# Sample y with C stationary on column groups, closer norm steps in the last scan unit, and pooling products of half 0 moved into the projection stage

## The chip, the cores and the metric

The kernel runs on one core of one Trainium2 chip. The core has five engines, each with an instruction queue of its own that is worked in order: TensorE (PE; its weight loads are shown as PEld), VectorE (DVE), ScalarE (ACT), GpSimd (POOL) and SyncE (SP), which here issues nearly all DMA transfers. The metric is the device time of one execution in microseconds; less is better. Before the change it is 2911.58 us, the median of 3 runs (2908.11 to 2915.21).

## The reference

One layer of a hybrid decoder trunk is computed in fp32 for 1024 prompt tokens (one sequence) and 64 sample tokens (8 sequences of 8 new tokens, each with a stored state). In short:

```python
x = x + 0.5 * swiglu(rmsnorm(x, norm_ffn1), ffn1_w_in, ffn1_w_out)
proj = rmsnorm(x, norm_mix) @ w_in            # u, z, x/B/C, dt, gate logits
d    = trailing_window_mean(u) - u            # windows 2, 4, 8, 16, one for each group of 256 channels
pool = (einsum('btgc,gcd->btgd', d, w_group) * pool_scale) @ pool_w_out
xs, B, C = silu(causal_conv(x/B/C))
y, state = ssd_scan(xs, dt, A, B, C, h0)      # h_t = exp(dt A) h_{t-1} + dt x_t B_t^T, y_t = h_t C_t
y = (y + d_skip * xs) * silu(z)
y = y * rsqrt(mean of y*y over each of 4 groups + eps) * ssd_norm
x = x + (sigmoid(g0) * pool + sigmoid(g1) * (y @ ssd_w_out)) @ w_o
x = x + 0.5 * swiglu(rmsnorm(x, norm_ffn2), ffn2_w_in, ffn2_w_out)
return rmsnorm(x, norm_final), and the new pool, conv and SSD states
```

The scan has 32 heads of 64 channels in 4 groups of 8 heads; each group has its own B and C of 128 states. For the prompt the state is zero at the start and the scan goes by chunks of 128 tokens. For a sample sequence the state comes in (64 x 128 for each head) and y of its 8 tokens has a part C h0, for each of 8 sequences and 32 heads.

## The kernel before

Activations lie with channels on partitions and tokens along the free dimension. The tokens are in two halves: half 0 is 512 prompt tokens, half 1 is 512 prompt tokens and the 64 sample tokens. A dense product is done in a split form: each fp32 operand is cut into a high and a low part (an ACT copy and a DVE subtraction, `split`), and three products high x high, low x high and high x low are summed in PSUM (`products`, L170 via `mm`). The FFN inputs and most of the projection use a Winograd-like form with seven block products (`wino`, tile pw).

There are four stages, each with its own SBUF and PSUM pools: the first FFN, the projection in its pools, the mix stage (opened by `open_stage("mix", ...)`), and the second FFN. A pool of a stage reuses the space of the one before, so its first tiles wait until the old ones have been read. A shared pool (`act`, 58 buffers of 128 x 576) lives through all of them. PSUM has 8 banks; in the mix stage 4 are for dense products (tag pd) and 4 for all the rest (tag ps).

**Order.** The program is written by a planner. `pe[0]` is its clock: each matmul adds max(columns, 64)/2400 us, four times that in plain fp32, and each transpose adds 0.107. The dense products are written in straight order; beside them run chains (Python generators), which yield a delay: the next piece of a chain is written when the clock has passed its due time (`tick`, `start`). `until(c)` and `finish(c)` write the rest of a chain at once. A list scheduler then fixes each engine's order from that program order and the dependences. Weights that were split and stored earlier (`plan`) are fetched 4 blocks ahead by `load_w` and `part_of`, on SP's queue.

**Mix stage.** The dense line is: pooling's grouped products and its output product for half 0 and half 1 (`mix_pool`, tiles pgm and pbp), the SSD output for half 0 in two parts of 8 rows (`ssd_out(0, 0)`, tile pso, then inside `mix_out(0)` the second part and the product with w_o, tile pwo), the same for half 1, and then the second FFN. Beside it runs the scan as one chain over 8 units (half, group), `scan` and `ssd_group`: for each chunk `ssd_a` (transposes pxT, decays, operand scaling), `ssd_b` (y, tiles pyo and pyd) and the state product pst. In half 1 each unit ends with a fifth chunk for the sample tokens: 8 state blocks (4 head pairs x 2 halves of the batch), each loaded, transposed on PE (ph0T), copied by ACT to h0T, multiplied with C (pyos) and updated with the new tokens' product (pnew).

When a unit ends, `gating` starts as a chain of its own: POOL multiplies with z, ACT squares, DVE adds, PE sums over partitions (pss), DVE takes the inverse root, PE transposes it (prt), it goes to DRAM and comes back on all partitions (rd, r), DVE scales y, and y is stored (yd). The delays between these are GP, G_WAIT and RD_WAIT; `ready[h]` counts stored groups. `y_load(h, q)` waits until the two groups of its part are ready, loads 8 rows of 128 channels and splits them (yh and y); it is started two or four column blocks before the `ssd_out` that uses it.

Before the mix stage, `first_pool` loads the 8 pooled tiles of half 0 (`pool_load`, name dd) and splits them (`pool_cut`, name dh) beside the last gate pair of the projection. In the second FFN, `operands` builds the Winograd operands of each half beside three plain products; T_AT holds the delay of its start, the last two entries for the second FFN.

Of the kernel before, what the change touches and what calls it, by code (L numbers as in the profile page):

```python
# [12 lines left out]
ALU = mybir.AluOpType  # L13
# [40 lines left out]
R_WAIT = 5.0  # L54
F_Y = 0.5
X1_AT = 4.0
T_AT, T_PACE = (2.0, 9.0, 25.0, 2.0), (1.5, 1.5)
DT_AT = 4.0
TURN_WAIT, UST_WAIT = 9.0, 9.0
TURN_AT, CONST_AT = 60.0, 40.0  # L60
HP, HP_ST = 40, 0
N_PRE = 3
Y_PACE = 0.8
G_WAIT = (5.0, 8.0)
H_AT, H_PACE, H_LAND, H_CUT = 1.0, (1.2, 0.9), (7.5, 4.5), 0.9
W_AT, W_NEXT = 108.0, 3.6
AHEAD = 4
# [4 lines left out]
def tile_hybrid_pool_ssd_macaron(  # L72
# [23 lines left out]
    def act(shape=(P, 576), dt=F32, name="a"):  # L96
        return sp.tile(list(shape), dt, tag="act", bufs=N_ACT, name=nm(name))
# [60 lines left out]
    def finish(c):  # L158
        while not c.done:
            c.step()  # L160
# [12 lines left out]
    def tr(out, in_, idn):  # L173
        T.transpose(out, in_, idn)
        pe[0] += 0.107
# [995 lines left out]
    dparts = {}  # L1171

    def pool_load(h, k):
        t = act((P, NTOK[h]), name="dd")
        dma(t, ddd[k][:, slice(*TOK[h])])
        dparts[h, k] = t

    def pool_cut(h, k):
        t = dparts[h, k]
        a = act((P, NTOK[h]), F32R, "dh")  # L1180
        split(t, a, t.bitcast(F32R))
        dparts[h, k] = a, t.bitcast(F32R)

    xn0 = []
    for k in range(KD):
# [45 lines left out]
    c = start(first_pool(), 0.5)  # L1231
    gate_pair(14, (1,))
    finish(c)
    st.close()


# [24 lines left out]
                dma(cdp[hh * HD : (hh + 1) * HD], csrc[hh].partition_broadcast(HD))  # L1261
        return t[:, :n], t[:, 160 : 160 + n], t[:, 320 : 320 + n], cd, (cdp, dtd3)

    def mix_pool(h):

        N, hs = NTOK[h], slice(*TOK[h])
        fh, fl = [None] * KD, [None] * KD

        def group(gi):
            dh, dl = zip(dparts.pop((h, 2 * gi)), dparts.pop((h, 2 * gi + 1)))  # L1270
            for j, pg in enumerate(dense2(wg[gi], 0, 0, [(h, dh, dl)], name="pgm")):
                m = gi * 2 + j
                fh[m], fl[m] = act((P, N), F32R, "fh"), act((P, N), F32R, "fl")
                for pt, (a, b) in zip(pg[0], PIECES[h]):
                    split(pt[:, : b - a], fh[m][:, a:b], fl[m][:, a:b], cols[:, i_ps + m : i_ps + m + 1])

        done = []

        def out(m):
            if done:  # L1280
                later(ACC_AT, lambda d=done.pop(): dma(*d))
            t0 = act((P, N), name="t0")
            dma(t0, gd[m][:, hs])
            pb = dense(wp, 0, KD, m * P, [(h, fh, fl)], name="pbp")[0]
            for pt, (a, b) in zip(pb, PIECES[h]):
                V.scalar_tensor_tensor(t0[:, a:b], t0[:, a:b], 1.0, pt[:, : b - a], op0=ALU.add, op1=ALU.mult)
            done.append((accd[h][m], t0))

        for gi in range(4):
            group(gi)  # L1290
        for m in range(KD):
            if h == 0 and m >= KD - 5:
                for k in range(2 * (m - KD + 5), min(KD, 2 * (m - KD + 5) + 2)):
                    pool_load(1, k)
                if m > KD - 5:
                    for k in range(2 * (m - KD + 4), 2 * (m - KD + 4) + 2):
                        pool_cut(1, k)
            if h == 1 and m == KD - 2:
                loads[0, 0] = start(y_load(0, 0))
            out(m)  # L1300
        dma(*done.pop())
# [40 lines left out]
            out.append((X3, bb))  # L1342
            yield STEP_S

    SAMPLE_UNITS = [(pr, bh) for pr in range(4) for bh in range(2)]

    def state_load(g, i):
        pr, bh = SAMPLE_UNITS[i]
# [67 lines left out]
    def ssd_b(h, g, c, a, hold, Cf, y4, dts, h0s):  # L1416

        dt, acs, dtd, cd, cdp = dts
        ab, xp, xd, ea, btok, L, tok = a[:7]
        smp = c == 4  # L1420
        ysl = y4[:, :, tok]
        first = h == 0 and c == 0
        if smp:
            po = psum("ps", "pyos")
            units, last = SAMPLE_UNITS, []

            def turn(h0, u):
                pt = psum("ps", "ph0T")
                for b in range(4):
                    tr(pt[:, b * P : (b + 1) * P], h0[:, b, :], ident)  # L1430
                hT = act((P, 4, P), name="h0T")
                S.copy(hT.rearrange("p b n -> p (b n)"), pt)
                gp = g * 4 + u[0]
                G.tensor_tensor(h0, h0, cdp[0][:, gp, u[1] * 4 : u[1] * 4 + 4].unsqueeze(2).broadcast_to([P, 4, P]), op=ALU.mult)
                return hT

            hTs = {0: turn(h0s[0], units[0])}
            for i, (pr, bh) in enumerate(units):
                if i + N_H0 < len(units):
                    h0s[i + N_H0] = state_load(g, i + N_H0)  # L1440
                yield STEP_S
                if i + 1 < len(units):
                    hTs[i + 1] = turn(h0s[i + 1], units[i + 1])
                hT, h0 = hTs.pop(i), h0s.pop(i)
                gp = g * 4 + pr
                for b in range(4):
                    bb = bh * 4 + b
                    mm(po[:, pr * L + bb * NT : pr * L + (bb + 1) * NT], hT[:, b, :],
                       Cf[:, 512 + bb * NT : 512 + (bb + 1) * NT])
                pn = psum("ps", "pnew")  # L1450
                mm(pn, xd[bh][0][:, pr * P : (pr + 1) * P], xd[bh][1].rearrange("p b n -> p (b n)"))
                V.tensor_tensor(h0.rearrange("p b n -> p (b n)"), h0.rearrange("p b n -> p (b n)"), pn, op=ALU.add)
                if len(last) > 1:
                    dma(*last.pop(0))
                dst = new_ssm_s[0, bh * 4 : bh * 4 + 4, 2 * gp : 2 * gp + 2].rearrange("b h p n -> (h p) b n")
                last.append((dst, h0))
            yield STEP_S
            for d in last:
                dma(*d)
        elif not first:  # L1460
            po = psum("ps", "pyo")
            for pr in range(4):
                mm(po[:, pr * L : (pr + 1) * L], hold[:, pr * P : (pr + 1) * P], Cf[:, tok])
        py = psum("ps", "pyd")
        for i in range(HPG):
            m_ = ab[:L, i, :]
            mm(py[(i % 2) * HD : (i % 2 + 1) * HD, (i // 2) * L : (i // 2 + 1) * L], xp[:L, i * HD : (i + 1) * HD], m_)
        pyv = py[:, : 4 * L].rearrange("p (q l) -> p q l", l=L)
        if first:
            V.tensor_tensor(ysl, ysl, pyv, op=ALU.add)  # L1470
        else:
            V.tensor_tensor(ea, po[:, : 4 * L].rearrange("p (q l) -> p q l", l=L), ea, op=ALU.mult)
            V.tensor_tensor(ea, ea, pyv, op=ALU.add)
            G.tensor_tensor(ysl, ysl, ea, op=ALU.add)

# [52 lines left out]
    def gating(h, g, y4, z4):  # L1528

        N = NTOK[h]  # L1530
        for j in range(4):
            G.tensor_tensor(y4[:, j, :N], z4[j], y4[:, j, :N], op=ALU.mult)
        yield GP[0]
        sq = [act((P, N), name="sq") for _ in range(4)]
        for j in range(4):
            S.activation(sq[j], y4[:, j, :N], AF.Square)
        yield GP[2]
        for j in range(1, 4):
            V.tensor_tensor(sq[0], sq[0], sq[j], op=ALU.add)
        sums = sq[:1]  # L1540
        rr = []
        yield from rstd(None, h, 512, rr, 1.0, sums, G_WAIT, RD_WAIT)
        for j in range(4):
            k = g * 4 + j
            y = y4[:, j, :N]
# [14 lines left out]

    def y_load(h, q):

        while ready[h] < 2 * q + 2:
            yield 1.0
        N = NTOK[h]
        parts = [], []
        for k in range(8 * q, 8 * q + 8):
            t, a = act((P, N), name="y"), act((P, N), F32R, "yh")
            dma(t, yd[h][k])
            parts[0].append(a)  # L1570
            parts[1].append(t)
            yield Y_LOAD
        yield 3.0
        for i in range(9):
            if i < 8:
                S.activation(parts[0][i], parts[1][i], AF.Copy)
            if i:
                a, t = parts[0][i - 1], parts[1][i - 1]
                V.tensor_tensor(t.bitcast(F32R), t, a.bitcast(F32), op=ALU.subtract)
            yield Y_PACE  # L1580
        return h, parts[0], [t.bitcast(F32R) for t in parts[1]]

    def scan():
# [97 lines left out]
        prep2.append((start(norm_parts(reload(0), 0, i_g2, o, PACE)), o))  # L1681
        return prep2[0][0]

    for h in HALVES:
        plan += [(w, 0, 2, 0, 2 * P) for w in wg]
        plan += [(wp, kb, 4, m * P, P) for m in range(KD) for kb in (0, 4)]
    for h in HALVES:
        plan += [(ws, q + kb, 4, m * P, P) for q in (0, 8) for m in range(KD) for kb in (0, 4)]
        plan += [(wz, kb, 4, m * P, P) for m in range(KD) for kb in (0, 4)]
    for h in HALVES:  # L1690
        plan += [(wi2, kb, 4, c0 + ff * P, P) for ff in range(N_PLAIN) for kb in (0, 4) for c0 in (0, FF)]
    start(scan())
    mix_pool(0)
    mix_pool(1)
    ssd_out(0, 0, (0, 1))
    mix_out(0, lambda: None, None)
    ssd_out(1, 0, (1, 1))
# [125 lines left out]
```

## Time and profile before

| | |
|---|---|
| median of 3 runs | 2911.58 us (2908.11 to 2915.21) |
| profiled execution, its own time | 2908.95 us |
| its span, first to last instruction | 2907.0 us |
| mean granted TensorE clock | 0.990 |
| PE busy | 2836.2 us, 98% of the span |
| DVE, ACT, POOL busy | 1635.7, 1316.6, 853.9 us |
| mix stage, from the last gate pair to the second FFN | about 1480 to 2150 us |

In the page and the views behind it, a row such as `PE MATMUL pyos<-Cf,h0T x256` names the engine, the operation, the tile written and the tiles read; buffer numbers are left out. An fp32 product shows as two records (two passes). Waits name what released an engine. In the view of busy time by stretch the column PEclk is the share of TensorE's full clock that was granted. In the chain of waits each line is a start, a length and what ran or was waited for.

### The profile page before, as it was taken

To read this page: it belongs to the slowest core of one execution; us is meant where nothing else is said; L and a number is where in the kernel's file an instruction comes from. 1 tells how busy PE (TensorE), PEld (TensorE's weight loads), DVE (VectorE), ACT (ScalarE), POOL (GpSimd) and SP (SyncE) were. 2 spreads that over 40 slices of the span, in tenths; PEclk is the share of its full clock that TensorE was granted. 3 is DMA by queue.
4 is the path that set the end of the run, shared out by engine and by line. 5 is a ranking of instruction groups with operands and counts; after the bars stand their busy time and mean duration, and the time that the engine had idled before them with its cause. 6 is when DMAs were issued, how large, how long until landed. Compare 5 with 4: busy or idle time off the path is not lost.

```text
span 2907.0 us, 54116 instructions
## 1 busy us (share of the span) xinstructions
PE 2836.2 (98%) x20338; PEld 2684.4 (92%) x20338; DVE 1635.7 (56%) x2839; ACT 1316.6 (45%) x2756; POOL 853.9 (29%) x913
## 2 busy tenths in 40 slices
PE   7999999999999999999999999999999999999998
PEld 6999999889999999999987887779999999998898
DVE  6556666544366877676458756762365433345532
ACT  5445545433244465555567745551223333344422
POOL 5333334110053333344214333431124333340100
PEclk9999999999999999999999999999999999999999
DMA  4489987755453333323378887886774222235542
GB/s 141 144 285 310 301 281 250 247 170 156 147 157 112 103 108 99 121 90 104 118 239 297 300 298 246 297 307 215 266 237 138 75 79 75 82 103 198 185 126 73
DMA packets 530520, 528.93 MB, mean 182 GB/s; under 512 B 43386, under 2 KB 372208, under 8 KB 530250
## 3 DMA queue, kind: packets, MB, share of 16 engines
q1 hardware_dynamic: 521846, 498.56, 53.0%
q0 software_dynamic: 7040, 24.52, 2.4%
q8 instruction: 160, 2.62, 0.4%
q10 hardware_dynamic: 1372, 2.40, 0.2%
q14 instruction: 102, 0.84, 0.1%
HBM read 374.73 MB, written 150.85 MB: 181 GB/s over the span
## 4 chain that ended last, share of the span: by engine, by line
PE 87%; DVE 6%; DMA 3%; ACT 2%; issue 1%; POOL 1%; SPq 0%; ACTq 0%; DVEq 0%; POOLq 0%
PE pw L170 48%; PE po L170 17%; PE pso L170 6%; PE pwo L170 3%; PE pbp L170 2%; PE pu L170 1%; PE pg L170 1%; PE pz L170 1%; PE pyos L170 1%; PE pyd L170 1%; PE pst L170 1%; DVE X L541 1%; PE ptx L170 1%; DMA r<-rd 1%; PE pyo L170 1%
## 5 line engine op out<-in xcount | busy, mean ns | idle before, releaser
L170 PE MATMUL pw<-hi,wl 128*128 128x288 f32 (+1 forms) x2176 | 628.8, 289 | 3.3 <-DVE wl L480 3.3
L170 PE MATMUL pw<-hi,wh 128*128 128x288 f32 (+1 forms) x2176 | 630.2, 290 | 0.0
L170 PE MATMUL pw<-lo,wh 128*128 128x288 f32 (+1 forms) x2176 | 627.8, 289 | 0.0
L170 PE MATMUL pw<-X,wh 128*128 128x256 f32 (+1 forms) x3264 | 623.5, 290 | 1.3 <-ACT rb L908 1.3
L170 PEld LDWEIGHTS pw<-X,wh 128*128 128x128 f32 x3264 | 516.0, 190 | 2.1 <-ACT rb L908 1.7
L170 PE MATMUL pw<-X,wl 128*128 128x256 f32 (+1 forms) x1632 | 471.0, 289 | 0.0
L170 PEld LDWEIGHTS pw<-hi,wl 128*128 128x128 f32 x2176 | 412.1, 189 | 4.3 <-DVE wl L480 4.3
L170 PEld LDWEIGHTS pw<-hi,wh 128*128 128x128 f32 x2176 | 412.3, 189 | 0.4
L170 PEld LDWEIGHTS pw<-lo,wh 128*128 128x128 f32 x2176 | 412.3, 189 | 0.0
L480 DVE TENSOR_TENSOR wl<-s,wh 128x512 fp32r<-128x512 f32 x284 | 205.0, 723 | 235.6 <-ACT wh L479 231.9
L473 POOL TENSOR_TENSOR s<-wraw,wraw 128x512 f32<-128x512 f32 x142 | 196.4, 1383 | 416.9 <-DVE wl L480 280.4
L170 PEld LDWEIGHTS pw<-X,wl 128*128 128x128 f32 x1632 | 310.9, 191 | 0.0
L479 ACT ACTIVATE wh<-s 128x512 fp32r<-128x512 f32 x284 | 179.3, 631 | 271.9 <-PE pw L170 217.2
L308 DVE TENSOR_TENSOR wl<-wraw,wh 128x512 fp32r<-128x512 f32 x216 | 143.8, 668 | 278.9 <-ACT wh L307 277.7
L170 PE MATMUL po<-hh,wh 128*128 128x288 f32 (+1 forms) x1056 | 289.2, 329 | 0.2 <-ACT wh L307 0.2
L170 PE MATMUL po<-hr,wh 128*128 128x288 f32 (+1 forms) x1056 | 288.0, 327 | 0.0
L170 PE MATMUL po<-hh,wl 128*128 128x288 f32 (+1 forms) x1056 | 288.0, 327 | 0.0
L307 ACT ACTIVATE wh<-wraw 128x512 fp32r<-128x512 f32 x216 | 128.7, 599 | 324.9 <-PE po L170 284.1
L479 ACT ACTIVATE wh<-wraw 128x512 fp32r<-128x512 f32 x213 | 134.4, 631 | 178.5 <-PE pw L170 156.1
L480 DVE TENSOR_TENSOR wl<-wraw,wh 128x512 fp32r<-128x512 f32 x213 | 156.9, 737 | 91.0 <-ACT wh L479 83.8
L170 PEld LDWEIGHTS po<-hh,wh 128*128 128x128 f32 x1056 | 179.3, 189 | 15.8 <-issue 1.7
L170 PEld LDWEIGHTS po<-hr,wh 128*128 128x128 f32 x1056 | 179.5, 188 | 14.0 <-DVE hr L383 0.5
(388 smaller groups left out, 5186.1 us busy)
## 6 DMA issues: line engine op xcount, KB each, us to landing
wraw<-in_ffn_w_in_dram SPq DMA_DIRECT2D x184, 256.0 KB
wraw<-wp SPq DMA_DIRECT2D x176, 256.0 KB
wraw<-in_ffn_w_out_dram SPq DMA_DIRECT2D x160, 256.0 KB
wraw<-in_w_in_dram SPq DMA_DIRECT2D x124, 256.0 KB
wp<-wp SPq DMA_DIRECT2D x88, 256.0 KB
wp<-wr SPq DMA_DIRECT2D x88, 256.0 KB
wh<-wp SPq DMA_DIRECT2D x88, 256.0 KB
wl<-wp SPq DMA_DIRECT2D x88, 256.0 KB
```

What stands on the lines that cost most here:

```text
L170: T.matmul(out, lhsT, rhs, start=start, stop=stop, skip_group_check=free)
L307: d = S.activation(wh, raw, AF.Copy)
L308: d2 = V.tensor_tensor(wl, raw, wh.bitcast(F32), op=ALU.subtract)
L473: G.tensor_tensor(t, a, b, op=op)
L479: S.activation(wh, a, AF.Copy)
L480: V.tensor_tensor(wl, a, wh.bitcast(F32), op=ALU.subtract)
L541: V.tensor_tensor(b, src, a.bitcast(F32), op=ALU.subtract)
```

## The change

1. **Sample y.** For each unit, `ssd_b` made four products with the transposed state of one sequence stationary (128 columns) and its 8 columns of C moving; the result lay with channels on partitions. Now 32 columns of C that hold those 8 are stationary, the transposed state moves (128 columns), and the four sequences of the unit write to the four groups of 32 partitions of one bank, which are four column groups of the array. The result lies with tokens on partitions. So units now go by batch half first and head pair second; after the four units of a batch half ACT copies the bank to SBUF (yt), four PE transposes turn it back (pyt), and DVE multiplies the 8 wanted columns of each 32 with the decay (`back`), for the first batch half during the second unit of the other one, for the second after the end. PSUM bank po is taken anew for each batch half.
2. **Last norm.** In the last unit (half 1, group 3) the delays of `gating` are shorter: 2.0 and 1.2 in place of 6.5 and 2.5, (2.0, 3.0) in place of (5.0, 8.0), and 3.0 in place of 6.0. `y_load` is now in two parts of 4 rows: each waits for its own group, loads, waits 3.0 and splits.
3. **Grouped products of half 0** are written at the end of the projection stage, ahead of `st.close()`, in its PSUM banks, by the new `pool_groups`; `mix_pool` gets their results. The dd tiles now come from the stage's own buffers (`fx`, which in the mix stage is the shared pool). The list of planned weight blocks is filled earlier, in the same order.
4. **Second FFN.** The operands of half 1 start at 9.0 instead of 2.0 on the planner's clock.

```diff
-T_AT, T_PACE = (2.0, 9.0, 25.0, 2.0), (1.5, 1.5)
+T_AT, T_PACE = (2.0, 9.0, 25.0, 9.0), (1.5, 1.5)
-G_WAIT = (5.0, 8.0)
+G_WAIT, G_LAST, GP_LAST = (5.0, 8.0), (2.0, 3.0), (2.0, 1.2)
...
     def pool_load(h, k):
-        t = act((P, NTOK[h]), name="dd")
+        t = fx(name="dd")[:, : NTOK[h]]
...
+    def pool_groups(h):
+
+        N = NTOK[h]
+        fh, fl = [None] * KD, [None] * KD
+        for gi in range(4):
+            dh, dl = zip(dparts.pop((h, 2 * gi)), dparts.pop((h, 2 * gi + 1)))
+            for j, pg in enumerate(dense2(wg[gi], 0, 0, [(h, dh, dl)], name="pgm")):
+                m = gi * 2 + j
+                fh[m], fl[m] = act((P, N), F32R, "fh"), act((P, N), F32R, "fl")
+                for pt, (a, b) in zip(pg[0], PIECES[h]):
+                    split(pt[:, : b - a], fh[m][:, a:b], fl[m][:, a:b], cols[:, i_ps + m : i_ps + m + 1])
+        return fh, fl
...
+    pooled = pool_groups(0)
     st.close()
...
-    SAMPLE_UNITS = [(pr, bh) for pr in range(4) for bh in range(2)]
+    SAMPLE_UNITS = [(pr, bh) for bh in range(2) for pr in range(4)]
...
+            def back(yt, bh):
+                pt = psum("ps", "pyt")
+                for q in range(4):
+                    tr(pt[:, q * P : (q + 1) * P], yt[:, q * P : (q + 1) * P], ident)
+                v = pt.rearrange("p (q b c) -> p q b c", q=4, c=32)[:, :, :, bh * 24 : bh * 24 + NT]
+                e = ea[:, :, bh * 32 : bh * 32 + 32].rearrange("p q (b t) -> p q b t", t=NT)
+                V.tensor_tensor(e, v, e, op=ALU.mult)
...
+                if pr == 0:
+                    po = psum("ps", "pyos")
                 for b in range(4):
-                    bb = bh * 4 + b
-                    mm(po[:, pr * L + bb * NT : pr * L + (bb + 1) * NT], hT[:, b, :],
-                       Cf[:, 512 + bb * NT : 512 + (bb + 1) * NT])
+                    t0 = 512 + bh * NT + b * NT
+                    mm(po[b * 32 : b * 32 + 32, pr * P : (pr + 1) * P], Cf[:, t0 : t0 + 32], hT[:, b, :])
+                if pr == 1 and ys:
+                    back(*ys.pop())
+                if pr == 3:
+                    yt = act((P, 512), name="yt")
+                    S.copy(yt, po)
+                    ys.append((yt, bh))
...
-        yield GP[0]
+        last = (h, g) == (1, NG - 1)
+        yield GP_LAST[0] if last else GP[0]
...
-        yield GP[2]
+        yield GP_LAST[1] if last else GP[2]
...
-        yield from rstd(None, h, 512, rr, 1.0, sums, G_WAIT, RD_WAIT)
+        yield from rstd(None, h, 512, rr, 1.0, sums, *((G_LAST, 3.0) if last else (G_WAIT, RD_WAIT)))
...
     def y_load(h, q):
-        while ready[h] < 2 * q + 2:
-            yield 1.0
...
+        for u in range(2):
+            while ready[h] < 2 * q + u + 1:
+                yield 1.0
+            for k in range(8 * q + 4 * u, 8 * q + 4 * u + 4):
...
-    mix_pool(0)
-    mix_pool(1)
+    mix_pool(0, *pooled)
+    mix_pool(1, *pool_groups(1))
```

More of the change, by code (lines that the diff above doesn't have):

```diff
@@ L1233, in tile_hybrid_pool_ssd_macaron @@
     finish(c)
+    for h in HALVES:
+        plan += [(w, 0, 2, 0, 2 * P) for w in wg]
+        plan += [(wp, kb, 4, m * P, P) for m in range(KD) for kb in (0, 4)]
+    for h in HALVES:
+        plan += [(ws, q + kb, 4, m * P, P) for q in (0, 8) for m in range(KD) for kb in (0, 4)]
+        plan += [(wz, kb, 4, m * P, P) for m in range(KD) for kb in (0, 4)]
+    for h in HALVES:
+        plan += [(wi2, kb, 4, c0 + ff * P, P) for ff in range(N_PLAIN) for kb in (0, 4) for c0 in (0, FF)]
+    pooled = pool_groups(0)
     st.close()
@@ L1262, in load_dts, with mix_pool @@
         return t[:, :n], t[:, 160 : 160 + n], t[:, 320 : 320 + n], cd, (cdp, dtd3)
-    def mix_pool(h):
+    def mix_pool(h, fh, fl):
         N, hs = NTOK[h], slice(*TOK[h])
[L1267 to L1275, printed above, removed]
         done = []
@@ L1287, in out @@
             done.append((accd[h][m], t0))
-        for gi in range(4):
-            group(gi)
         for m in range(KD):
@@ L1423, in ssd_b @@
         if smp:
-            po = psum("ps", "pyos")
-            units, last = SAMPLE_UNITS, []
+            po = None
+            units, last, ys = SAMPLE_UNITS, [], []
+            def back(yt, bh):
[5 more added lines that the diff above has]
+                V.tensor_tensor(e, v, e, op=ALU.mult)
             def turn(h0, u):
@@ L1459, in ssd_b @@
                 dma(*d)
+            back(*ys.pop())
         elif not first:
@@ L1471, in ssd_b @@
         else:
-            V.tensor_tensor(ea, po[:, : 4 * L].rearrange("p (q l) -> p q l", l=L), ea, op=ALU.mult)
+            if not smp:
+                V.tensor_tensor(ea, po[:, : 4 * L].rearrange("p (q l) -> p q l", l=L), ea, op=ALU.mult)
             V.tensor_tensor(ea, ea, pyv, op=ALU.add)
@@ L1561, in y_load @@
     def y_load(h, q):
-        while ready[h] < 2 * q + 2:
-            yield 1.0
         N = NTOK[h]
         parts = [], []
[L1567 to L1580, printed above, removed]
+        for u in range(2):
+            while ready[h] < 2 * q + u + 1:
+                yield 1.0
+            for k in range(8 * q + 4 * u, 8 * q + 4 * u + 4):
+                t, a = act((P, N), name="y"), act((P, N), F32R, "yh")
+                dma(t, yd[h][k])
+                parts[0].append(a)
+                parts[1].append(t)
+                yield Y_LOAD
+            yield 3.0
+            for i in range(4 * u, 4 * u + 5):
+                if i < 4 * u + 4:
+                    S.activation(parts[0][i], parts[1][i], AF.Copy)
+                if i > 4 * u:
+                    a, t = parts[0][i - 1], parts[1][i - 1]
+                    V.tensor_tensor(t.bitcast(F32R), t, a.bitcast(F32), op=ALU.subtract)
+                yield Y_PACE
         return h, parts[0], [t.bitcast(F32R) for t in parts[1]]
@@ L1682, in prep_a2 @@
         return prep2[0][0]
[L1684 to L1691, printed above, removed]
     start(scan())
-    mix_pool(0)
-    mix_pool(1)
+    mix_pool(0, *pooled)
+    mix_pool(1, *pool_groups(1))
     ssd_out(0, 0, (0, 1))
```

## The prediction

> **What bounds the kernel now.** I read the page's header first, then the busy time by stage, the waits of TensorE (PE), the granted clock in slices of 5 us, and last the chain of waits where those views pointed.
>
> ```profile
> span 2907.0 us, 54116 instructions
> ...
> PE 2836.2 (98%) x20338; PEld 2684.4 (92%) x20338; DVE 1635.7 (56%) x2839; ACT 1316.6 (45%) x2756; POOL 853.9 (29%) x913
> ```
>
> ```profile
> core 0: us, PE busy (x) PEld busy (x) DVE busy (x) ACT busy (x) POOL busy (x), PEclk, DMA share, GB/s
> 1000.00:1480.00 480.00, 478.38 (x3797) 475.32 (x3796) 320.53 (x577) 267.41 (x526) 174.66 (x240) 1.00 0.36 110
> 1500.00:1700.00 200.00, 188.73 (x1314) 157.72 (x1315) 157.48 (x270) 148.34 (x340) 64.73 (x51) 0.98 0.90 309
> 1700.00:2000.00 300.00, 290.19 (x1779) 245.16 (x1778) 181.05 (x293) 136.18 (x310) 109.36 (x86) 0.94 0.81 272
> 2000.00:2150.00 150.00, 140.49 (x1028) 139.03 (x1028) 56.51 (x108) 30.10 (x52) 15.57 (x13) 0.97 0.74 253
> ```
>
> PE is the bound. In the projection stage (1000 to 1480 us) it is full and at full clock. In the mix stage (1480 to 2150) it is not: some 30 us idle between 1500 and 2150, and a granted clock of 0.94 and 0.97. So a term can be won in three ways there: less PE work, a PE wait that goes, or a half-speed stretch that goes.
>
> ```profile
> PE pso L170 <- ACT yh L1576: 8.6, 1, 8.6
> PE pgm L170 <- DVE fl L385: 4.0, 3, 2.1
> PE pu L170 <- ACT g L452: 2.6, 1, 2.6
> ...
> PE prt L174 <- DVE rsm L396: 1.8, 3, 1.2
> ...
> PE pyos L170 <- ACT h0T L1432: 1.2, 2, 0.8
> ```
>
> Each edit has one of these rows: the last scan unit's norm the first, the grouped products the second, the later start of the second FFN's operands the third; the last two rows are what the neighbours of the added waits cost now.
>
> **Sample y (pyos).** Before, each of 32 units makes 4 fp32 products with a 128-column stationary state and 8 moving columns; they are recorded as two passes each.
>
> ```profile
> L170 PE MATMUL pyos<-Cf,h0T x256: 170/256/363, 1701.4 to 1976.9; 128*128 128x8 f32 x128
> ```
>
> ```profile
> 1965.78 0.44 PE ph0T L174 x4
> ...
> 1966.97 0.79 PE pyos L170 x8
> ```
>
> A unit's 8 records take 0.79 us, 99 ns each: it is the loading of 128 stationary columns that is paid, not the 8 moving ones. After, C is stationary (32 columns), the state moves (128 columns), and the four batches of a unit go to four column groups. The trace has no such product with 128 moving columns, but has two neighbours: pdt, 32-column stationary on four column groups with 288 moving, and the sample's pyd, two groups with 64 moving.
>
> ```profile
> 816.95 0.42 PE L170 MATMUL pz<-hi,wraw 128*128 128x288 f32 x2
> 817.30 2.15 PE L170 MATMUL pdt<-x,wdt 128*32 128x288 f32 x32
> ...
> 819.38 0.53 PE L170 MATMUL pz<-hi,wraw 128*128 128x288 f32 x2
> ```
>
> ```profile
> 1522.87 1.02 PE pyd L170 x16
> ...
> 1810.27 0.61 PE pyd L170 x16
> ```
>
> The two pz records before pdt use 0.13 us each, so PE was free for pdt at 817.21 and free again at 819.38: 2.17 us for 32 records, 68 ns each. One after the other, at the rate of the rows above, 288 columns in a pass of fp32 would take about twice pz's 0.13 us; so four groups do run together (0.26/4 = 65 ns), and the change of tile shape costs some 0.1 to 0.25 us in all. The 64-column pyd shows that a record can cost 38 ns (0.61/16). Low bound for the new unit: 128/288 of 65 ns = 29 ns, times 8, plus 0.25 = 0.48 us. High bound: the 128-column pyd at 64 ns (1.02/16), times 8, plus 0.25 = 0.76 us. Near pdt I take 0.5: gain 0.29 x 32 = 9.3 us (0.9 to 9.9).
>
> New on PE are 4 transposes for each half of a group, 32 in all; 4 of the same kind take 0.44 us (ph0T), so 3.5 us. ACT gets 8 copies of 128x512 and VectorE 8 small products for 4 larger ones; both are under half busy from 1700 to 2000 (136 and 181 of 300 us), which hides them. Net **5.8 us**, from -2.6 to +6.4; if the groups did not overlap at all (8 x 0.11 + 0.25 = 1.13 us a unit) it would be -14.4.
>
> [...]
>
> **The clock around it.** Half-speed stretches stand at the dense parts of the four sample groups (the last row is for a later part):
>
> ```profile
> 1715.00:1720.00 5.00, 5.00 (x30) 4.61 (x28) 3.36 (x6) 2.11 (x4) 2.00 (x2) 0.66 0.65 198
> 1720.00:1725.00 5.00, 5.00 (x20) 4.43 (x20) 2.01 (x4) 2.15 (x4) 1.04 (x1) 0.50 0.26 77
> 1725.00:1730.00 5.00, 5.00 (x30) 4.38 (x30) 3.00 (x6) 2.13 (x4) 2.64 (x3) 0.50 0.90 249
> 1790.00:1795.00 5.00, 4.29 (x17) 3.57 (x18) 1.94 (x4) 0.00 (x0) 0.00 (x0) 0.67 0.29 90
> 1895.00:1900.00 5.00, 5.00 (x25) 4.21 (x22) 2.77 (x3) 1.63 (x3) 4.01 (x4) 0.50 1.01 278
> 1975.00:1980.00 5.00, 5.00 (x35) 4.76 (x35) 2.19 (x4) 0.65 (x2) 1.66 (x3) 0.50 1.00 283
> ...
> 2040.00:2045.00 5.00, 5.00 (x25) 5.00 (x25) 4.22 (x6) 3.35 (x5) 0.00 (x0) 0.58 0.72 283
> ```
>
> One minus the clock, times 5 us, summed over the first six rows: 1.7 + 2.5 + 2.5 + 1.65 + 2.5 + 2.5 = 13.4 us of full speed missing. They come where 8-column products and transposes follow each other with little dense work between. With 128 moving columns the same units stream more, and they shift against the dense work (below), out of the knot at 1715 where pso waits for its first operands. Whether this lifts the clock cannot be read from before: 0 to 13.4; I take half, **7 us**.
>
> [...]
>
> **Grouped products of half 0.** Before, they are the first PE work of the mix stage and their copies stand in ACT's queue behind the scan's first scaling, which waits for a load that waits for the last store of the stage before:
>
> ```profile
> 1492.99 3.53 DMA gd<-rb
> ...
> 1497.01 4.66 DMA xs<-cv
> ```
>
> ```profile
> 1494.00 0.69 ACT L381 ACTIVATE fh<-pgm,cols 128x512 fp32r<-128x512 f32 x1 [1.03 <-PE pgm L170]
> 1500.73 0.72 ACT L1498 ACTIVATE y<-xs,Dcol 128x512 f32<-128x512 f32 x1 [6.05 <-DMA xs<-cv]
> ...
> 1502.32 0.67 ACT L381 ACTIVATE fh<-pgm,cols 128x512 fp32r<-128x512 f32 x1
> ```
>
> ```profile
> 1492.30 0.50 PE L170 MATMUL pgm<-dh,wh 128*128 128x512 f32 x1 [0.54 <-ACT rb L920]
> ...
> 1499.02 0.39 PE L170 MATMUL pgm<-dh,wl 128*128 128x512 f32 x1
> ...
> 1512.13 0.51 PE L170 MATMUL pbp<-fh,wh 128*128 128x512 f32 x1 [0.69 <-DVE fl L385]
> ```
>
> From the end of the gate pair (1492.30 less 0.54 idle, 1491.8) to the first pbp is 20.3 us. The work in it is 48 products at 0.23 us (the two pgm rows are the first and the 30th: 6.72/29), 11.0, plus two scan steps' transposes and small products, which I estimate from ph0T's 0.44 for four at 2.4 in all: so 7 us are lost. Moved ahead of the stage's end, the copies are in ACT's queue before the scan's, and pbp follows at once. Against it: the eight dd tiles now lie in the stage's own buffers, so the scan's loads may start only when the last grouped product has read them, near 1502.7 instead of 1496.6; SP's queue is in order, and behind them wait the pooling weights. Four blocks are fetched ahead, 48 products or 11 us, which covers that. If this cover fails, it costs the 6 us. I take **5 us**, from -3 to +7.
>
> **The last unit's norm.** The scan ends here while pso of half 1 runs, and PE then runs dry:
>
> ```profile
> 1977.29 1.05 PE pyd L170 x16
> ...
> 2005.16 24.80 PE pso L170 x186
> ...
> 2031.96 5.76 DMA y<-yd
> ...
> 2038.57 6.55 PE pso L170 x28
> ```
>
> From 2029.96 to 2038.57 PE waits: 8.6 us, and it restarts at half clock (0.58 from 2040 to 2045, 2.1 us more). The planner's delays in this chain go from 6.5 + 2.5 + 5 + 8 + 6 = 28 to 11.2; that is 16.8 of its microseconds, and a matmul of 288 columns that it counts as 0.12 takes 0.133 (24.80/186), so 18.6 us. The grouped products of half 0 no longer stand beside the scan, which brings the need forward by 11. The load of y in two parts leaves 4 rows instead of 8 behind the last norm: 4 x (0.6 + 0.8) x 1.11 = 6.2 us. 18.6 - 11 + 6.2 = 13.8, more than the 8.6 needed. The first four rows are there long before, and 24 products (3.2 us) cover the others. What is late next is the transpose of the norm on PE (prt), now 3 instead of 8 behind its sums, with VectorE's small steps (rsm) between: at most the 1.2 us of its row. Of 8.6 + 2.1 I take **9 us**, 0 to 10.7.
>
> **Later combine in the second FFN.** The 2.6 us wait for g stands behind operand splits of half 1; 7 us later they meet other work. **2 us**, 0 to 2.6.
>
> **What it costs elsewhere.** PE's queue is in order, and each of the 8 transposed blocks waits there for a copy on ACT; the nearest row is pyos behind h0T, 1.2 us for 2 waits of 32. The split load of y is longer in the planner (2 x (2.4 + 3 + 4) = 18.8 against 4.8 + 3 + 7.2 = 15.0) where readiness is no limit, and for the first pso it starts two columns of 48 products ahead, 11.5, so its second four rows come late. Together **-5 us**, from -12 to 0.
>
> Sum: 5.8 + 7 + 5 + 9 + 2 - 5 = 23.8. The profiled execution's own time is 2908.95 (span 2907.0 and 2 us around it): 2885.2. The median of the runs is 2.6 above that execution, so **2887**.
>
> **The rivals.** (a) *The column groups bring nothing and the clock stays low.* For it: the 64 ns records, and the transposes; against: pdt. Pyos -2.6, clock 0: -2.6 + 5 + 9 + 2 - 5 = 8.4, so 2903. (b) *The end's wait stays*, because 11 us of cover left the scan, or because loads stand behind weights in SP's queue: 23.8 - 9 = 14.8, so 2897. For it: the load of y was issued only at 2031.96, behind all the products ahead of it in the order, and the scheduler may again leave it last. (c) *All of it comes*: 6.4 + 13.4 + 7 + 10.7 + 2.6 = 40, so 2871. (d) *Slower*: one mechanism, PE standing at each transposed block while ACT finishes what is ahead of the copy. It decides when the 8 blocks cost more than the rest brings, 28.8/8 = 3.6 us each; at 4.5 us each, 36 in all, the time is 2919. Against it: the h0T row has the same form and is far shorter.
>
> **How the numbers follow.** Chances: forecast 0.50, (a) 0.20, (b) 0.14, (c) 0.09, (d) 0.07. The forecast's own range is 2876 to 2898. To leave no more than 2 in 10 outside, the range goes down nearly to (c) and up to (a): 2871 to 2905. No change means within 0.2%, 5.8 us, which is what a measurement here can tell. The forecast, (b) and (c) are faster but for 0.02; (a) is 0.14 faster and 0.06 same; (d) 0.01 same. So faster 0.85, same 0.09, slower 0.06.
>
> **What would show it.** Pyos near 0.5 us for 8 records; clock slices of 1.00 around the sample groups; pgm of half 0 without a gap and pbp right behind; no pso wait for yh over 2 us; pu's wait for g gone. Wrong it would be by a new PE wait at the transposed blocks for yt, or by a first pso that waits longer for its second four rows.

## The result, and the profile after

The changed kernel takes 2889.22 us (median of 4 runs, 2887.1 to 2892.7). The kernel before, run beside it, takes 2909.85 us. The ratio is 0.993, with a 95% interval of 0.9909 to 0.9951: the change makes the kernel faster by 14 to 26 us. The profiled execution has a span of 2888.7 us, 18.3 less than before. One later execution of c1_count_only (4621.64 us, at a granted clock of 0.555) and one of the kernel before (5586.86 us) are in no figure below.

The head of the page of the changed kernel:

```profile
span 2888.7 us, 54171 instructions
...
PE 2818.7 (98%) x20370; PEld 2650.9 (92%) x20370; DVE 1637.6 (57%) x2843; ACT 1321.4 (46%) x2764; POOL 860.1 (30%) x913
```

PE is still the bound, and the span fell by about what its busy time fell (17.5 us). The page does not say where. For that I cut both traces at the same points of the work: the end of the projection's last product, the first pbp, the first pso, the first pso of half 1, its second part, the first pwo of half 1, and the first Winograd product of the second FFN. Busy time by stretch, of the kernel before (the stretch in us from the span's start, its length, busy time and records of each engine, granted clock, DMA share, GB/s):

```profile
1491.80:1512.10 20.30, 16.39 (x64) 12.14 (x64) 5.24 (x8) 12.80 (x24) 0.00 (x0) 0.92 1.00 343
1512.10:1718.00 205.90, 197.44 (x1419) 168.82 (x1419) 158.43 (x273) 141.02 (x327) 70.58 (x57) 0.99 0.90 308
1718.00:1963.40 245.40, 235.59 (x1379) 191.39 (x1378) 162.96 (x255) 123.97 (x286) 93.05 (x71) 0.95 0.82 277
1963.40:2039.50 76.10, 67.48 (x489) 66.63 (x487) 16.61 (x34) 13.84 (x31) 10.46 (x9) 0.90 0.67 226
2039.50:2092.70 53.20, 53.20 (x385) 53.20 (x385) 21.30 (x36) 8.55 (x13) 10.00 (x7) 0.96 0.71 235
2092.70:2220.60 127.90, 124.43 (x837) 117.85 (x836) 74.06 (x132) 38.91 (x77) 36.78 (x38) 1.00 0.67 225
```

The same view of the changed kernel, cut at the same points:

```profile
1493.80:1506.90 13.10, 11.39 (x50) 8.95 (x49) 7.49 (x11) 7.10 (x12) 0.00 (x0) 1.00 0.83 275
1506.90:1714.50 207.60, 194.17 (x1374) 163.98 (x1374) 158.13 (x267) 147.03 (x338) 69.07 (x52) 0.98 0.87 306
1714.50:1964.00 249.50, 239.75 (x1565) 178.82 (x1564) 168.57 (x274) 132.16 (x301) 103.35 (x82) 0.99 0.87 291
1964.00:2025.90 61.90, 55.48 (x402) 55.20 (x400) 18.02 (x31) 13.22 (x31) 6.17 (x4) 0.94 0.73 246
2025.90:2076.30 50.40, 50.40 (x381) 50.40 (x380) 17.78 (x30) 5.92 (x9) 9.98 (x7) 1.00 0.78 261
2076.30:2202.20 125.90, 124.93 (x838) 118.70 (x837) 73.71 (x132) 38.50 (x77) 37.63 (x39) 1.00 0.68 229
```

| stretch | before | after | difference |
|---|---|---|---|
| boundary, to the first pbp | 20.3 | 13.1 | -7.2 |
| pooling | 205.9 | 207.6 | +1.7 |
| pso and pwo of half 0, first part of half 1 (with sample y) | 321.5 | 311.4 | -10.1 |
| second part of half 1 | 53.2 | 50.4 | -2.8 |
| pwo of half 1 and the start of the second FFN | 127.9 | 125.9 | -2.0 |

The third and fourth rows are added up because the end of the scan moved across the cut between them; the scan's last product, a transpose of the final state (pfin), starts at 1979.0 before and at 1962.0 after. The sum is -20.4; the projection ended 2.0 later in this execution, which gives the span's -18.3.

The rows that answer to those of the prediction. Waits of PE, changed kernel (total, times, longest):

```profile
PE pss L170 <- DVE sq L1567: 6.6, 2, 6.4
...
PE pbp L170 <- DVE fl L385: 2.4, 2, 1.6
...
PE pso L170 <- DVE y L1608: 1.6, 2, 0.9
...
PE pu L170 <- DVE g L608: 0.5, 1, 0.5
...
PE pyt L174 <- DVE h L1477: 0.4, 1, 0.4
```

The two waits that the prediction wanted gone are gone: pso for yh (8.6) and pu for ACT's g (2.6). The first row is new, 6.4 us in one piece: the sums over partitions of the last norm wait for VectorE.

Sample y, the groups of its products and transposes, and two pieces of the chain of waits:

```profile
L170 PE MATMUL pyos<-h0T,Cf x256: 272/297/423, 1713.4 to 1958.8; 128*32 128x128 f32 x128
...
L174 PE MATMUL pyt<-ident,yt x32: 270/273/328, 1729.7 to 1960.8; 128*128 128x128 f32 x32
```

```profile
1727.08 0.36 PE pyos L170 x8
...
1729.65 0.66 PE pyt L174 x4
```

A unit's 8 records take 0.36 us, 45 ns each, where they took 0.79. Granted clock of the changed kernel in slices of 5 us, all six below 0.9 between 1480 and 2050 and three at places that were slow before:

```profile
1590.00:1595.00 5.00, 2.94 (x14) 2.71 (x15) 5.00 (x7) 4.15 (x9) 3.13 (x3) 0.74 0.65 235
1595.00:1600.00 5.00, 4.72 (x28) 3.88 (x27) 2.42 (x5) 4.26 (x12) 0.00 (x0) 0.58 0.00 0
1715.00:1720.00 5.00, 2.66 (x9) 1.54 (x8) 4.24 (x7) 0.37 (x1) 1.08 (x1) 0.87 0.68 214
1720.00:1725.00 5.00, 5.00 (x27) 3.57 (x27) 0.69 (x1) 0.59 (x1) 1.04 (x1) 0.79 1.05 318
1725.00:1730.00 5.00, 4.59 (x45) 2.89 (x44) 1.38 (x2) 2.31 (x4) 2.70 (x3) 1.00 0.50 160
1790.00:1795.00 5.00, 5.00 (x41) 3.40 (x40) 1.92 (x3) 0.59 (x1) 2.17 (x3) 1.00 0.70 204
1895.00:1900.00 5.00, 5.00 (x24) 4.12 (x23) 2.08 (x4) 4.50 (x13) 1.27 (x2) 1.00 1.03 377
1970.00:1975.00 5.00, 1.87 (x9) 1.89 (x10) 2.88 (x4) 1.26 (x2) 0.17 (x1) 0.63 0.85 275
1975.00:1980.00 5.00, 5.00 (x28) 4.94 (x29) 1.95 (x13) 0.26 (x1) 0.00 (x0) 0.69 0.04 14
```

One minus the clock, times 5 us, summed over the slow slices (the clock lost, below): 8.5 us, of which 3.4 around the new wait of pss (last two rows). The same sum over the kernel before, from 1480 to 2050, is 25.5. The sum counts slices in which PE partly stands idle too, so it is the most that the lower clock can have cost. At the sample groups the full clock is back, but for 1.7 us from 1715 to 1725.

### The profile page after: what moved, and what is told of

It reads as the page before. It is cut to its first block, busy times and chain, and to the rows that moved or that the text cites. A ratio compares the mean times of both kernels' runs of the same rounds, so it can differ in the third digit from the quotient of the medians.

```text
span 2888.7 us, 54171 instructions
## 1 busy us (share of the span) xinstructions
PE 2818.7 (98%) x20370; PEld 2650.9 (92%) x20370; DVE 1637.6 (57%) x2843; ACT 1321.4 (46%) x2764; POOL 860.1 (30%) x913
## 4 chain that ended last, share of the span: by engine, by line
PE 88%; DVE 5%; DMA 2%; ACT 2%; issue 1%; POOL 0%; SPq 0%; ACTq 0%; DVEq 0%; POOLq 0%
PE pw L170 49%; PE po L170 18%; PE pso L170 6%; PE pwo L170 3%; PE pg L170 2%; PE pu L170 2%; PE pbp L170 1%; PE pz L170 1%; PE pst L170 1%; PE pyd L170 1%; PE pgm L170 1%; DVE y L1574 1%; PE ptx L170 1%; PE pyo L170 1%; PE pss L170 0%
## 5 line engine op out<-in xcount | busy, mean ns | idle before, releaser
L170 PEld LDWEIGHTS po<-hh,wl 128*128 128x128 f32 x1056 | 179.4, 188 | 14.2 <-DVE wl L308 0.4
```

What stands on the lines that cost most here:

```text
L170: T.matmul(out, lhsT, rhs, start=start, stop=stop, skip_group_check=free)
```

## The experiments

Each was timed against the kernel before on the same chip; s1 to s4 ran on one chip, b1, b3, b4 and c1 on a second, c2, b2 and d1 on a third. "Clock lost" is the sum just explained, from 1480 to 2050 us, of one profiled execution each.

| label | what it is | median us | ratio to before (95%) | clock lost |
|---|---|---|---|---|
| s1_sample_y | before + sample y alone | 2882.0 | 0.9898 (0.988 to 0.9916) | 5.1 |
| s2_norm | before + closer norm and y in two parts | 2906.31 | 0.9982 (0.9971 to 0.9994) | 15.4 |
| s3_pool | before + grouped products moved | 2913.2 | 1.0009 (0.9999 to 1.002) | 18.8 |
| s4_t_at | before + later operands | 2908.2 | 0.9993 (0.9981 to 1.0004) | 30.7 |
| b1_sums_11 | changed, last norm's sums 9 later | 2881.86 | 0.9901 (0.9883 to 0.992) | 1.7 |
| b3_no_norm | changed without the norm edit | 2888.75 | 0.9922 (0.9905 to 0.9939) | 10.2 |
| b4_no_pool | changed without the moved products | 2886.81 | 0.9918 (0.9902 to 0.9934) | 8.6 |
| c1_count_only | before, sample units counted longer | 2901.2 | 0.997 (0.9957 to 0.9983) | 11.9 |
| c2_old_count | sample y alone, counted as before | 2889.34 | 0.9926 (0.9913 to 0.9938) | 8.5 |
| b2_y_t_at | before + sample y + later operands | 2880.28 | 0.9891 (0.9874 to 0.9908) | 6.8 |
| d1_no_pool_sums | changed, no moved products, sums 9 later | 2877.65 | 0.9887 (0.9872 to 0.9901) | 3.4 |

How much of a difference in clock lost is chance can be read from s4. Its 20338 PE records come in the same order as those of the kernel before, yet it loses 30.7 us where the kernel before loses 25.5. So 5 us here mean nothing. What stands clear is that the eight kernels with the new sample product, the changed one among them, lose 1.7 to 10.2 us, and the five with the old one 11.9 to 30.7.

**One part at a time (s1 to s4).** Each is the kernel before with the hunks of one part of the diff; for the last:

```diff
-T_AT, T_PACE = (2.0, 9.0, 25.0, 2.0), (1.5, 1.5)
+T_AT, T_PACE = (2.0, 9.0, 25.0, 9.0), (1.5, 1.5)
```

> The kernel before with the sample y edit alone. In the changed kernel's trace a unit's 8 records take about 0.40 us against 0.79 before, 12.5 us over 32 units, less 3.5 us for 32 transposes: 9 us. Theory A (the wider moving operand also lifts the clock): the half-speed slices around the sample groups between 1700 and 1985 us mostly go, up to 13 us more, so 9 to 20 us faster, 2890 to 2901. Theory B (the clock came back in the changed kernel because the sample groups were shifted against the dense work by the other edits): the knot at 1715 to 1730 keeps its half clock, and the gain is 5 to 9 us, 2901 to 2905. The 8.6 us wait of pso for yh at the end stays in both.

> The kernel before with the closer norm steps of the last scan unit and the load of y in two parts. Theory A: the wait of pso for yh (8.6 us and 2.1 us of half clock behind it) goes and nothing comes in its place: 10 us faster, 2900. Theory B (from the changed kernel, where PE waits 6.4 us for the squares' sum, pss behind DVE sq): the closer steps put the sum over partitions ahead of its data, and about 6 us of the 10 come back as a wait of pss: 3 to 5 us faster, 2905 to 2907.

> The kernel before with the grouped products of half 0 moved into the projection stage alone. At the stage's boundary about 5 us are won (last pw to first pbp, less the scan's work in it). Theory A: the 11 us of dense work that no longer stand beside the scan bring the need for y at the end forward, so the wait of pso for yh grows from 8.6 to about 19 us: 4 to 7 us slower in all, 2914 to 2917. Theory B: the wait at the end does not grow, since the scan is not bound to that work: 5 us faster, 2905.

> The kernel before with the later start of the operands of half 1 in the second FFN alone. Theory A: the 2.6 us wait of pu for g goes, nothing else moves: 2.6 us faster, 2907. Theory B: the operand work meets the first wide products instead, and a wait of pw for X or of ACT for POOL takes its place: within 1 us of before.

Sample y alone is worth 1.02% (0.84 to 1.2), some 30 us, more than the whole change. The norm alone brings 0.18% (0.06 to 0.29), about 5 us. The moved products and the later operands cannot be told from nothing. By their ratios the four singles add up to 34 us where the change brings 20, so the parts get in each other's way. Waits of PE with sample y alone, with the norm alone and with the moved products alone:

```profile
PE pu L170 <- ACT g L452: 2.0, 1, 2.0
...
PE pso L170 <- ACT yh L1593: 1.2, 1, 1.2
```

```profile
PE pss L170 <- DVE sq L1540: 5.3, 1, 5.3
```

```profile
PE pso L170 <- ACT yh L1586: 8.5, 1, 8.5
PE pss L170 <- DVE sq L1549: 6.5, 2, 5.1
```

With sample y alone the 8.6 us wait for yh shrinks to 1.2, although nothing of the norm was touched. With the norm alone the wait for yh goes, and pss waits 5.3 us in its place. With the products moved alone the wait for yh stays at 8.5 and pss waits as well, at the old delays.

Of these four expectations only s2's theory B came true. Both theories of s1 missed: they kept the 8.6 us wait, and the time is below both ranges. In s3 the wait for yh neither grew to 19 us, as A had it, nor did the kernel get faster, as B had it. In s4 the wait of pu for ACT's g went, as A had it, but the time lies between the two and cannot be told from before.

**Why does sample y end the wait for yh (c1, c2)?** The planner counts the new unit 0.43 us longer (4 products of 128 columns instead of 64, plain fp32), and a chain's next step is due its delay after the clock at which the step before began (`self.due = pe[0] + (next(self.gen) or 0.0)`, L136, where `pe[0]` is read first). So a unit that counts longer leaves less of its 1.6 us delay for dense products. In PE's order in the traces the scan's last tile (pfin) stands behind 1322 dense products of the mix stage before, and behind 1285 with sample y. c1 keeps the old product and only counts more (1298), c2 has the new product and counts as before (1316):

```diff
+                pe[0] += 4 * 64 / 2400.0 * 4
```

```diff
+                    pe[0] -= 4 * 64 / 2400.0 * 4
```

> The kernel before with its old sample product, only the planner's count for the four products of a unit raised by 0.43 us to that of the new form. Theory A (the wider moving operand itself lifts the clock and shortens the unit): the half-speed slices around the sample groups stay or grow, and only the wait of pso for yh shrinks because the scan ends about 24 products earlier: 2903 to 2909. Theory B (what sample y brings comes mostly from the planner's count, which places the units otherwise): the half-speed slices go and the kernel is 12 us or more faster, 2900 or less.

> Sample y alone, but the planner's clock counts each of its 32 units as short as the old ones (0.43 us less than its own count), so that the scan's steps keep their old distance and its last tile stands behind 1316 dense products of the mix stage as before (1322), not behind 1285. Theory: the whole product without the count gives the shorter units only, 32 x (0.79 - 0.40) = 12.5 us less 32 transposes at 0.11 = 3.5, so 9 us off 2910, and perhaps 5 to 10 us of granted clock: 2891 to 2901. Rival, the wide product itself lifts the clock and ends the wait for yh, the count is a side matter: 2882 as in the kernel with sample y alone, clock lost between 1480 and 2050 us near 5 us. Tells apart: the wait of pso for yh (over 4 us by the theory, under 2 by the rival).

The count alone, with not one instruction more or less on PE, gives 0.3% (0.17 to 0.43), about 9 us. The product alone gives 0.74% (0.62 to 0.87), about 21.5. Together they make up the 30 of sample y. c1 lies between its two theories: the time fits neither, and slow slices still stand at the end of its last sample group and behind it (1960 to 1975: 0.79, 0.50, 0.69). Its wait for yh, stage row and clock slices:

```profile
PE pso L170 <- ACT yh L1577: 3.1, 2, 1.8
```

```profile
1700.00:2000.00 300.00, 290.13 (x1853) 244.40 (x1852) 184.49 (x297) 138.26 (x313) 110.32 (x87) 0.98 0.83 279
...
1715.00:1720.00 5.00, 5.00 (x44) 4.92 (x43) 2.71 (x5) 1.70 (x3) 2.08 (x2) 1.00 0.81 258
1720.00:1725.00 5.00, 5.00 (x48) 4.31 (x47) 3.34 (x6) 2.75 (x5) 2.08 (x2) 1.00 0.52 155
1725.00:1730.00 5.00, 4.15 (x20) 3.10 (x19) 4.65 (x7) 2.68 (x5) 3.56 (x3) 1.00 0.83 237
```

The stretch from 1715 to 1730 is at full clock with the old 8-column products (those of the first sample group from 1710 on stand at 1710.6 to 1724.0); it was 0.66, 0.50, 0.50. This is one execution, of 2896.52 us, 4.7 below the median of c1. Over all 11 the mean granted clock is 0.9935, against 0.991 in the 17 of the kernel before beside it, some 7 us of a span. The same slices of c2, with the new product counted as before:

```profile
1715.00:1720.00 5.00, 5.00 (x56) 3.16 (x55) 3.55 (x8) 2.73 (x5) 2.70 (x3) 1.00 1.02 337
1720.00:1725.00 5.00, 5.00 (x47) 3.77 (x46) 4.24 (x8) 3.42 (x7) 1.37 (x2) 1.00 0.64 194
1725.00:1730.00 5.00, 3.29 (x13) 1.86 (x13) 4.34 (x3) 1.49 (x3) 4.92 (x4) 1.00 0.89 274
```

So 128 moving columns are not what the clock needs there. Nor does c1's trace prove that it was the count: s2, with the old product and the old count, has no slow slice there either (its nearest is 1735 to 1740, 0.68). Waits of PE in c2:

```profile
PE pss L170 <- DVE sq L1557: 4.1, 1, 4.1
...
PE pso L170 <- ACT yh L1594: 2.8, 3, 1.2
```

Neither theory of c2 holds as it stood: the time, 2889.34, lies between the two that they gave, and so does the wait for yh (2.8 us in three pieces). The wait for yh gives up most of its 8.6 us by the product too, and c2 pays 4.1 of it back to pss. The last pfin starts at 1979.0 us before, at 1969.0 in c1, at 1957.9 in c2 and at 1957.2 in s1; that the shorter work ahead of it is what brings it forward in c2 fits these starts, but was not tried by itself. The two parts of sample y nearly add, and each is more than its instructions.

**What holds the changed kernel back (b1, b3, b4, d1, b2).** b1 moves only the sums of the last norm to a later place in the order; b3 and b4 leave out one part; d1 is b4 with b1's edit; b2 is s1 with the later operands.

```diff
-G_WAIT, G_LAST, GP_LAST = (5.0, 8.0), (2.0, 3.0), (2.0, 1.2)
+G_WAIT, G_LAST, GP_LAST = (5.0, 8.0), (11.0, 3.0), (2.0, 1.2)
```

> The changed kernel with one number changed: the sums over partitions of the last norm are written 11.0 instead of 2.0 after the squares. Theory A (the closer steps put pss 11 us of data latency ahead of its sums, and PE pays 6.4 us there and about 3 us of half clock behind it): the wait of pss for DVE sq goes, no wait of pso for yh takes its place because the last loads of y had some 10 us to spare, and the kernel is 6 to 9 us faster than the changed one: 2880 to 2883. Theory B (the wait only moves on to the load of y): pso waits for yh by about the same, 2887 to 2890.

> The changed kernel without the closer norm steps and without the load of y in two parts (sample y, pooling and the second FFN's start stay). Theory A (the norm edit costs more than it brings once sample y is in, and pooling moved is neutral): like sample y alone or a little better, 2878 to 2884, with pss not waiting. Theory B (without the 11 us of cover the load of y is late again): a wait of pso for yh of 6 to 10 us, 2887 to 2892.

> The changed kernel with the grouped products of half 0 left in the mix stage (sample y, norm edit and the second FFN's start stay). Theory A: the wait of pss for its sums (about 6 us) is there without the pooling edit too, so the kernel is near sample y alone plus 6 less 2, 2884 to 2888. Theory B (it is the pooling edit that spoils what sample y brings): 2878 to 2882.

> The kernel before with sample y and the later operands of the second FFN alone. If the two add up: the wait of pu for g (2.0 us with sample y alone) goes, and 2882.0 becomes 2880. If the later start was only a shift of the wait: 2882, with another PE wait of about 2 us in the second FFN.

> The changed kernel without the moved grouped products and with the last norm's sums 9 planner microseconds later (the wait before them 11.0 in place of 2.0). Theory (sums too early, everything else of the norm edit harmless): the 5.3 us wait of pss for sq goes as it went with the moved products in place (2889.2 to 2881.9), and from 2886.8 the time comes to 2880. If the moved products in truth bring 4 us once the sums are no longer too early: 2884 or more, above the 2881.9 of the kernel that has them.

What ends last before the sums is plain in the changed kernel's own order of time, POOL, then (after ACT's squares) VectorE, then PE:

```profile
1963.09 7.08 POOL L1559 TENSOR_TENSOR y<-z,y 128x576 f32<-128x576 f32 x4
...
1971.56 0.75 DVE L1608 TENSOR_TENSOR y<-y,yh 128x576 fp32r<-128x576 f32 x1
1972.23 0.75 DVE L1567 TENSOR_TENSOR sq<-sq,sq 128x576 f32<-128x576 f32 x1
...
1973.13 2.14 PE L170 MATMUL pss<-ones,sq 128*128 128x1 f32 x10 [6.42 <-DVE sq L1567]
```

The four products with z take POOL 7.08 us, the last addition ends 9.9 us after the first of them starts, and the planner's delays to the sums are 2.0 + 1.2 + 2.0 = 5.2. PE reaches pss, finds no sums, and stands. The last 1.4 us before the last addition are VectorE's own queue: ACT's last square ended at 1970.88, and a split of a row of y (L1608) stood ahead. With the sums 9 later (b1, as its theory A had it) this wait and the lower clock around it go (clock lost 8.5 to 1.7), a wait for yh of 1.8 comes back, and the time falls from 2889.22 to 2881.86. The ranges of the two do not touch (2880.12 to 2883.2 against 2887.1 to 2892.7), though the intervals of their ratios overlap by a thousandth. Without the norm edit altogether (b3) the time is 2888.75, the same as with it: the edit in its early form wins nothing here. That time is in the range of b3's theory B, but the wait that B gave for it is not there: pso waits 1.2 us for yh, pss 2.3 for sq. b4 came as its theory A had it, with pss waiting 5.3 us in one piece.

The moved products. In each of the four pairs that differ in them alone the kernel that has them has the higher median. s3 cannot be told from the kernel before, nor the changed kernel from b4 (the ranges overlap by 0.83 us). Between b1 and d1, with the sums put right, it is 4.2: 2880.12 to 2883.2 against 2876.89 to 2880.55, an overlap of 0.43. Between b3 and b2 it is 8.5, and the ranges are apart: 2883.84 to 2889.54 against 2877.26 to 2881.66. The last two pairs ran on different chips, and the intervals of the ratios overlap. The 2884 or more that d1 was to take if the moved products bring 4 us did not come. So they cost here rather than bring; how much is not fixed. The pooling stretch of b1, three of PE's waits in it, and the same stretch of d1:

```profile
1507.80:1714.10 206.30, 192.63 (x1374) 162.84 (x1374) 157.83 (x267) 147.07 (x338) 69.13 (x52) 0.99 0.87 306
```

```profile
PE pst L170 <- ACT ab L1398: 1.9, 3, 1.0
...
PE pst L170 <- DVE xp L1405: 1.2, 1, 1.2
PE pst L170 <- DVE xd L1402: 1.0, 1, 1.0
```

```profile
1513.50:1714.80 201.30, 192.85 (x1397) 162.73 (x1398) 159.92 (x271) 142.91 (x330) 69.98 (x56) 0.99 0.89 307
```

With the products moved the boundary is 7.6 us shorter (13.3 against 20.9), but PE idles 13.7 us in the pooling stretch instead of 8.4, and the next two stretches are 6.3 us longer together. The three waits of pst, the scan's state product, add up to 4.1 in b1; in d1 pst waits 0.4 in this stretch. Pbp's wait for fl is 2.4 against 0.7. A reading of this is that the scan's first steps had those 48 products beside them as cover and now do not. It reads the waits; no run put other cover beside the scan.

b2 and s1 differ by 1.7 us, inside their intervals; the wait of pu for ACT's g is gone in b2, as expected. b2 is also the corner from which the rest of the change can be built up: the norm edit added to it gives b4, the moved products b3, both the changed kernel.

| | products left | products moved |
|---|---|---|
| old norm steps | 2880.28 (b2) | 2888.75 (b3) |
| norm edit as built | 2886.81 (b4) | 2889.22 (changed) |
| norm edit, sums 9 later | 2877.65 (d1) | 2881.86 (b1) |

Once sample y is in, the norm edit as built costs 6.5 us by itself (2884.74 to 2887.93, apart from b2), the moved products 8.5, and both together 8.9; b2 and d1 ran on another chip than b3, b4 and b1, and the intervals of b2's ratio and those of b3 and b4 overlap by less than 0.001. With its sums late the norm edit wins 6.9 us where the products are moved, and cannot be told from nothing where they are not (d1 and b2 overlap). d1 is the fastest of all, 0.9887 (0.9872 to 0.9901): 33 us below the kernel before, against 20 for the change.

## Why the prediction was right, point by point

The total was right: 2887 predicted (the sum gives 2887.8), 2889.22 measured, inside the forecast's own range. The terms were not: five of six were off, and their errors cancelled. Sample y and the clock brought more than I gave them, the norm edit and the moved products nothing or a loss; that the total came out within 2 us is luck.

**Sample y, net 5.8 us, from -2.6 to +6.4: too small, bounds included.** The step that failed is the 0.25 us for the change of tile shape, which both bounds contain. The unit's 8 records take 0.36 us, below the low bound of 0.48. Two passes at pdt's rate are an estimated 0.23, so at most 0.13 is left for the change. By this row the units save 0.43 x 32 = 13.8, less the transposes. The chain's four pyt take 0.66 where I counted 0.44, so 3.5 to 5.3 for the 8 blocks, and the net is 8.5 to 10.3. The pdt row was the right neighbour; of the 0.1 to 0.25 us that I read from it as the price of the tile shape I took the upper end, and the lower one was nearer.

**The clock, 7 us, from 0 to 13.4: right that it lifts, too small, and the cause stays open.** Of the six slow slices that I summed (13.4), the same places now lose 3.3; over the whole stage it is 25.5 to 8.5, with the 5 us of chance said above. I named two causes, more streaming columns and the shift against the dense work. The stretch from 1715 to 1730 is at full clock in c1 with the shift alone, in c2 with the product alone, and in s2 with neither (1.00 in all three slices of each). What sets the clock back there stays open. The 32 new transposes, which rival (a) had on its side, did not keep the clock low: with them it was 0.99 from 1480 to 2150 us, where it had been 0.96, and no run here shows what they do by themselves.

**Sample y also ended the tail, which I had not seen at all.** I costed the edit as instructions only. In a kernel that is written out by a planner it is also a count, and the count moved the scan's end from product 1322 to 1285. That is 37 products, 4.9 us at 0.133. In c1 the count alone moved it by 24, the wait for yh fell from 8.6 to 3.1, and with what it gave in granted clock it is worth about 9 us.

**Grouped products of half 0, 5 us, from -3 to +7: the boundary did as told, the sum did not.** It shrank by 7.2 us, pgm ran without a gap, and the first pbp came after 1.56 us of idle. Changed kernel, last grouped copy on ACT and first pbp on PE:

```profile
1505.36 0.69 ACT L381 ACTIVATE fh<-pgm,cols 128x512 fp32r<-128x512 f32 x1 [0.70 <-PE pgm L170]
```

```profile
1506.88 0.50 PE L170 MATMUL pbp<-fh,wh 128*128 128x512 f32 x1 [1.56 <-DVE fl L385]
```

The failed step is "so 7 us are lost": 5.0 of the 7.2 are busy time of PE (16.39 and 11.39), and only 2.2 were idle. Some 1.6 of the 5.0 is the lower clock (0.92 over 20.3 us), the rest work of the scan's first steps, which only moved; I had estimated that work at 2.4 where it is over 3. And I named the cover of the loads, but not what the 48 products themselves were covering. Alone the edit measures 1.0009 (0.9999 to 1.002), no gain, and b3 against b2 is 8.5 us slower.

**The last norm, 9 us, from 0 to 10.7: right on the wait, wrong on what is late next.** The wait for yh went. The failed sentence is "what is late next is the transpose of the norm on PE (prt) ... at most the 1.2 us of its row". Late was pss, one step earlier: 6.4 us, and at most 3.4 of lower clock around it, against the 8.6 + 2.1 removed. Added to b2, where pso waits only 1.2 us for yh, the edit costs 6.5 (b4). I compared the planner's delays with how much had to be won (13.8 against 8.6), and never with how long the chain behind them runs on POOL, ACT and VectorE.

**Later combine, 2 us: right as a mechanism, and in its stretch in size.** The wait of pu for ACT's g (2.6) is gone; the 0.5 for VectorE's g was there before too. The stretch from the first pwo of half 1 to the first Winograd product takes 127.9 and 128.0 us without the edit (before, s1) and 125.9, 125.4 and 125.7 with it (changed, b1, d1). Alone the edit measures 0.9993 (0.9981 to 1.0004), which holds both 2 us and nothing.

**Elsewhere, -5 us: wrong in its reason.** Behind ACT's copies PE did not stand: the waits of pyt add up to 0.4 us, and their row names VectorE, so rival (d) had nothing to it. The first pso's waits for its rows are 1.6. The -5 covered instead, by chance, the new wait of pss and the idle in the pooling stretch.

Rival (b) came half true: the end's wait did stay, in another tile. Rival (c), all of it at 2871, is not reached even by d1 at 2877.65. The signs that I named would have said so early: pyos at half its old time, most slices at 1.00 and no yh wait all came, and only the row that I had not named, pss, tells why the gain stops at 20.

## What to carry to other kernels

Where a planner writes the order, cost an edit twice, as engine time and as the change of the planner's clock: here the same products counted longer were worth 9 us. Before delays are shortened, add up the engine rows of the chain behind them; here delays of 5.2 us ahead of a chain of 9.9 became a PE wait of 6.4 us at pss, with the next products of pso behind it. And before dense work is moved out of a stage, ask what it was covering there.

## What the runs showed of the hardware

Four column groups with 32 stationary and 128 moving columns in plain fp32 take 45 ns a record (0.36 us for 8), where 128 stationary and 8 moving columns took 99 ns (0.79 us for 8). By the row of pdt (68 ns a record, an estimated 65 without the change of tile shape) a pass of 288 columns takes an estimated 0.26 us for all four groups. So 128 columns would be an estimated 0.116, and the two passes 0.23: by this estimate the unit pays up to 0.13 us beyond that.

Slices at a granted clock of 0.50 stood where PE was recorded busy for all 5 of 5 us (before, 1720 to 1725 and 1895 to 1900), and in c1's trace, with the same instructions at another spacing, both places are at 1.00. Even one order of instructions does not fix it: from 1875 to 1893 the third sample group of the kernel before had a clock of 1.00, and the same records in s4 (1878 to 1900) had 0.80 (0.61, 0.71, 1.00 and 0.82 in the four slices from 1880 to 1900). So on this kernel neither busy time nor the kind of products alone tells when the clock is halved.
